# A two-layer hybrid backbone on one core: the first layer's modulation weights regrouped by feature, and its first four token tiles multiplied part by part

## The chip, the core and the metric

The kernel runs on one core of a Trainium2 chip. The metric is device microseconds (us) of one execution, and the number for a kernel is the median of its runs. All work is float32: each operand of a large matrix product is split into a rounded part `h` and the rest `l`, and a product is three matmuls (`h*h`, `h*l`, `l*h`).

## The reference

Two layers run over 1024 latent tokens and 256 context tokens of width 1024. What matters here is the start of the first layer: a modulation vector from the condition, a normalised and modulated input, and the projection that feeds three head groups.

```python
def hybrid_layer(x, xc, c, c_ctx, lp, lambda_init, rope_a, rope_b, ctx_out):
    mod = jax.nn.silu(c) @ lp['w_mod'] + lp['b_mod']            # 1024 -> 6 * 1024
    mod_c = jax.nn.silu(c_ctx) @ lp['w_mod'] + lp['b_mod']
    sh1, sc1, g1, sh2, sc2, g2 = [m[:, None] for m in jnp.split(mod, N_MOD, axis=-1)]
    h = modulate(rms_norm(x, lp['norm1_gain']), sh1, sc1)       # h * (1 + sc1) + sh1
    hc = modulate(rms_norm(xc, lp['norm1_gain']), sh1c, sc1c)
    aq, ak, av, bq, bk, bv, cx, cg = jnp.split(h @ lp['w_in'], split_pts, axis=-1)
    ...
```

`aq, ak, av` feed differential attention, `bq, bk, bv` windowed attention, `cx, cg` a gated linear recurrence (LRU). After them come an output projection, a second norm and a gated MLP. All of that is the same in both kernels.

## The kernel before, in words

Tokens lie along the free axis in three chunks `CH` (0 to 511, 512 to 1023, and the 256 context tokens); features lie in eight blocks of 128 partitions, `KC = 8`. `phase_a` (L432) does a layer's norm, projection and LRU. For the first layer it goes so:

- `load` (L442) brings x of chunk 1, eight transfers of 256 KB. `norm_scale` (L381) squares it on ACT (`nacc`, `nsq`, L364 and L367), adds the squares on DVE and POOL (L369, L390), sums over partitions with four small matmuls (`n_col`, L392), takes the power -1/2 on POOL (`nr`, L396) and spreads the result over partitions with four transposes into a PSUM bank (`n_bc`, L399).
- `mod_first` (L304) is called four times. A call loads four 512 KB tiles `wmod` (512 output columns for all 1024 inputs), multiplies them (L302), copies the result to SBUF (`m`, L313), transposes it (`mod_t`, L291), and writes four column blocks of the table `mods` with a reduction (L293) and an addition of the bias (L296). Columns 0 to 7 of `mods` are the shifts of the eight feature blocks, 8 to 15 their scales, so all four calls are needed before any block has both.
- `affine` (L345) makes `amul = (1 + scale) * gain` for all blocks with two DVE instructions (L353, L354).
- `norm_apply` (L402) makes, for each block of a chunk, `ntm` on DVE (L411: x times `amul` times `n_bc`), `hh` on ACT (L417, or L413 and L184), and the rest `hl` on DVE (L418) or, for blocks 1, 4 and 6, on POOL (L187).
- `weight` (L189) loads 512 KB into one of two buffers `raw`, rounds it on ACT (L184) and takes the rest on POOL (L187). The four weights `ws` of the group `wg2` and `wx` of the LRU go through it.
- `qkv` (L625) multiplies one tile of 128 tokens by `ws`: 24 matmuls of 512 columns into one of four PSUM banks `qkv_ps` (L636 to L638), then `qk_post` (L655) normalises and rotates the result on ACT, DVE and POOL (its first read of the bank on DVE is L670). `lru` (L543) makes `cx` with 72 matmuls in three pieces (L427 to L429), then convolves, gates and scans.

`lru_consts` (L515) computes, for both layers in `setup`, constants from the parameters: a chain of small DVE instructions in a buffer of the tag `raw`.

The order is not the written one: the whole of `phase_a` stands in a block that the framework schedules by its own timeline (L278), engine by engine. Every engine then takes its own list strictly in order.

Of the kernel before, what the change touches and what calls it, by code (L numbers as in the profile page):

```python
# [19 lines left out]
DEPTH = 2  # L20
# [45 lines left out]
def prep(i):  # L66
# [11 lines left out]
    out["wmod"] = i["w_mod"].reshape(L, 4, 2, P, 12, 512).transpose(0, 4, 1, 3, 2, 5).reshape(L, 12, 4, P, 1024)  # L78
# [92 lines left out]
class Build:  # L171
# [17 lines left out]
    def weight(self, src, n=1024):  # L189
        nc = self.nc  # L190
        raw = self.big.tile([P, 1024], F32, tag="raw", name="raw", bufs=2)
# [37 lines left out]
    def setup(self):  # L229
# [9 lines left out]
        mk = self.big.tile([P, 1024], F32, tag="raw", name="mask_f", bufs=2)  # L239
        nc.sync.dma_start(mk[:, 0:384], self.a["cst"][:, 132:516])  # L240
        self.hi(self.mask, mk[:, 0:384])
# [10 lines left out]
        for l in range(DEPTH):  # L252
            p = self.cst.tile([P, NPRM], F32, name=f"prm{l}")
            nc.sync.dma_start(p, self.a["prm"][l])
            self.prms.append(p)
            self.modl.append(self.cst.tile([P, 48, 2], F32, name=f"mods{l}"))
            self.lru_consts(l)
# [7 lines left out]
        self.ud = self.dr.tile([NF, P, T], F32, name="ud")  # L265

# [19 lines left out]
    def mod_out(self, l, nb, m4):  # L286

        nc = self.nc
        pt = self.ps_t("mod_t")
        for j in range(4):  # L290
            nc.tensor.transpose(pt[:, P * j:P * j + P], m4[:, P * j:P * j + P], self.ident)  # L291
        out = self.modl[l][:, 4 * nb:4 * nb + 4, :]
        nc.vector.tensor_reduce(out, pt.rearrange("p (j g r) -> p j r g", j=4, g=4)[:, :, 0:2, :], AX.X, ALU.add)  # L293
        o, n = PRM["bmod"]
        bm = self.prms[l][:, o + 4 * nb:o + 4 * nb + 4]
        nc.vector.tensor_tensor(out, out, bm.unsqueeze(2).to_broadcast([P, 4, 2]), ALU.add)  # L296
# [7 lines left out]
    def mod_first(self, l, nb):  # L304
        nc = self.nc
        ps = self.psp.tile([P, 512], F32, tag="p", name="mod_ps")
        for a in range(4):
            raw = self.big.tile([P, 1024], F32, tag="h", name="wmod", bufs=16)
            nc.sync.dma_start(raw, self.a["wmod"][l, nb, a])
            for s in range(2):  # L310
                self.mod_mm(ps, 2 * a + s, raw[:, 512 * s:512 * s + 512], a < 2, a >= 2)
        m4 = self.s5("m4")
        nc.scalar.activation(m4, ps, AF.Copy)  # L313
        self.mod_out(l, nb, m4)
# [30 lines left out]
    def affine(self, which, l=None):  # L345
        nc = self.nc
        l = self.l if l is None else l
        mods = self.modl[l]
# [1453 lines left out]
```

## Time and profile before

| | us |
|---|---|
| runs | 3084.51, 3085.17, 3091.09 |
| median | 3085.17 |
| the profiled execution | 3091.96 |
| its span, first to last instruction | 3089.4 |
| PE busy (share of the span) | 2840.6 (92%) |
| DVE busy | 2060.3 (67%) |
| ACT busy | 1450.4 (47%) |
| POOL busy | 1513.6 (49%) |

PE is the matrix engine, PEld its weight loads, DVE the vector engine, ACT the scalar engine, POOL the general engine, SP the one that issues nearly all transfers. The shares are means over the whole span; the change lies in its first 175 us, so the rows further down are of that stretch.

### The profile page before, as it was taken

The numbers are of one execution on the slowest core, as the hardware profiler recorded it, in microseconds if no ns is written. First come the engines' busy times: TensorE is split into PE (matmuls) and PEld (weight loads), VectorE is DVE, ScalarE is ACT, GpSimd is POOL, SyncE is SP. The second block draws the span as 40 slices with busy tenths as digits, with TensorE's granted clock in tenths as the row PEclk, the third lists the DMA queues.
The fourth block names the chain that finished last, engine by engine and source line by source line (L and its number), as shares of the span: only waits on it lengthen the run. The fifth ranks groups of instructions, "written<-read, shape, count | busy, mean of one in ns | idle before, by whom it ended". The sixth has DMA issues, their size and how long they took to land. (4 is left out here: it accounts for less than half of the span.)

```text
span 3089.4 us, 40964 instructions
## 1 busy us (share of the span) xinstructions
PE 2840.6 (92%) x15146; PEld 2307.3 (75%) x15146; DVE 2060.3 (67%) x2879; ACT 1450.4 (47%) x2410; POOL 1513.6 (49%) x1011
## 2 busy tenths in 40 slices
PE   6999798999899999998988989898999799999898
PEld 4798665768688888886777778666777678887776
DVE  6956556775855444457887884756885755555997
ACT  5444366785444344343332444466883444444331
POOL 4645412323555444439562664612323566665981
PEclk9999999999999999999999999899999999999999
DMA  7232636664121121143215341454534122224322
GB/s 252 81 85 79 167 67 219 196 212 158 51 81 67 68 74 67 67 169 125 82 49 200 103 113 52 118 135 148 138 118 146 55 82 82 84 85 159 122 83 82
DMA packets 208279, 349.25 MB, mean 113 GB/s; under 512 B 32720, under 2 KB 112336, under 8 KB 208080
## 3 DMA queue, kind: packets, MB, share of 16 engines
q1 hardware_dynamic: 203472, 331.69, 33.2%
q0 software_dynamic: 4608, 14.95, 2.2%
q8 instruction: 119, 1.95, 0.3%
q14 instruction: 80, 0.66, 0.1%
HBM read 257.19 MB, written 89.39 MB: 112 GB/s over the span
## 5 line engine op out<-in xcount | busy, mean ns | idle before, releaser
L184 ACT ACTIVATE w_r<-w_raw 128x512 fp32r<-128x512 f32 x338 | 213.0, 632 | 447.1 <-PE u_ps L1550 276.8
L1522 POOL TENSOR_TENSOR w_raw<-w_raw 128x512 f32<-128x512 f32 x176 | 250.9, 1430 | 226.8 <-DVE w_r L187 105.5
L187 DVE TENSOR_TENSOR w_r<-w_raw,w_r 128x512 fp32r<-128x512 f32 x206 | 149.4, 728 | 250.3 <-ACT w_r L184 250.2
L1549 PE MATMUL u_ps<-a,w_r 128*128 128x512 f32 x704 | 278.3, 396 | 5.2 <-DVE vb L1637 4.0
L1550 PE MATMUL u_ps<-a,w_r 128*128 128x512 f32 x704 | 277.5, 394 | 1.4 <-DVE a L187 1.2
L1551 PE MATMUL u_ps<-a,w_r 128*128 128x512 f32 x704 | 275.9, 392 | 0.0
L187 POOL TENSOR_TENSOR w_r<-w_raw,w_r 128x512 fp32r<-128x512 f32 x132 | 190.7, 1445 | 119.2 <-ACT w_r L184 114.0
L1401 PE MATMUL d_ps<-d_ah,d_b 128*128 128x512 f32 x560 | 224.7, 402 | 22.3 <-DVE xd L1378 10.9
L1402 PE MATMUL d_ps<-d_al,d_b 128*128 128x512 f32 x560 | 224.5, 401 | 6.2 <-DVE d_al L187 6.2
L1403 PE MATMUL d_ps<-d_ah,d_b 128*128 128x512 f32 x560 | 223.5, 399 | 0.7 <-DVE d_b L187 0.7
L944 DVE TENSOR_REDUCE da_sm<-da_s 128x1 f32<-128x1280 f32 (+1 forms) x144 | 194.9, 1368 | 42.8 <-PE da_s L934 42.0
L187 POOL TENSOR_TENSOR w<-raw,w 128x1024 fp32r<-128x1024 f32 (+2 forms) x62 | 140.7, 2276 | 145.1 <-ACT w L184 136.5
L951 ACT ACTIVATE da_e<-da_s,da_sm 128x1280 f32<-128x1280 f32 (+1 forms) x144 | 177.6, 1235 | 24.7 <-DVE da_sm L944 22.7
L1549 PEld LDWEIGHTS u_ps<-a,w_r 128*128 128x128 f32 x704 | 133.7, 190 | 34.8 <-DVE vb L1637 5.6
L1088 POOL TENSOR_TENSOR oy_x<-oy_x,oy_z 128x426 f32<-128x426 f32 (+3 forms) x48 | 52.1, 1085 | 217.6 <-ACT oy_z L1086 189.3
L1550 PEld LDWEIGHTS u_ps<-a,w_r 128*128 128x128 f32 x704 | 133.8, 190 | 29.7 <-DVE a L187 2.1
L1551 PEld LDWEIGHTS u_ps<-a,w_r 128*128 128x128 f32 x704 | 133.5, 190 | 28.6
L1378 DVE SCALAR_TENSOR_TENSOR xd<-d_ps,mods,xd 128x512 f32<-128x512 f32 x200 | 140.9, 741 | 18.9 <-PE d_ps L1403 18.8
L1401 PEld LDWEIGHTS d_ps<-d_ah,d_b 128*128 128x128 f32 x560 | 108.9, 195 | 47.7 <-issue 9.1
L934 PE MATMUL da_s<-dak,daq 96*128 96x512 f32 (+1 forms) x400 | 123.0, 395 | 14.9 <-ACT da_e L951 14.5
L1637 DVE TENSOR_TENSOR vb<-u_ps,vb 128x512 f32<-128x512 f32 x96 | 66.1, 688 | 99.4 <-PE u_ps L1551 90.5
L1402 PEld LDWEIGHTS d_ps<-d_al,d_b 128*128 128x128 f32 x560 | 108.9, 194 | 30.2 <-DVE d_al L187 8.0
(347 smaller groups left out, 8589.6 us busy)
## 6 DMA issues: line engine op xcount, KB each, us to landing
wmod<-in_wmod SPq DMA_DIRECT2D x96, 512.0 KB, 6.5
w_raw<-in_wu SPq DMA_DIRECT2D x44, 1024.0 KB, 5.4
d_w<-in_wd SPq DMA_DIRECT2D x40, 512.0 KB, 3.9
d_a<-ud SPq DMA_DIRECT2D x40, 512.0 KB, 4.7
ud<-conv SPq DMA_DIRECT2D x22, 640.0 KB, 2.9
ud<-conv SPq DMA_DIRECT2D x22, 512.0 KB, 2.6
raw<-in_wg SPq DMA_DIRECT2D x16, 512.0 KB, 4.4
dak<-qk_da POOLq DMA_DIRECT2D x48, 160.0 KB, 4.5
```

The costliest lines, as they stand in the source:

```text
L184: self.nc.scalar.activation(out, in_, AF.Copy)
L187: (eng or self.nc.vector).tensor_tensor(out, in_, hi.bitcast(F32), ALU.subtract)
L944: nc.vector.tensor_reduce(st["sm"][:, mi:mi + 1], st["s"][mi][:, :b["nkc"]], AX.X, ALU.max, negate=True)
L951: nc.scalar.activation(e[:, :nkc], st["s"][mi][:, :nkc], AF.Exp, bias=st["sm"][:, mi:mi + 1], accum_out=b["s0"][:, ti, u["hd"], mi:mi + 1])
L1378: nc.vector.scalar_tensor_tensor(x, ps, gate, x, ALU.mult, ALU.add)
L1401: nc.tensor.matmul(ps, bh[:, w], ah[:, m], start=on is None and k == 0, stop=False, **kw)
L1402: nc.tensor.matmul(ps, bh[:, w], al[:, m], start=False, stop=False, **kw)
L1403: nc.tensor.matmul(ps, bl[:, w], ah[:, m], start=False, stop=k == 1, **kw)
L1522: sub = lambda o, a, b, op=ALU.subtract: nc.gpsimd.tensor_tensor(o, a, b, op)
L1549: nc.tensor.matmul(ps, wh[:, s], h, start=new and kk == 0, stop=False, skip_group_check=not new)
L1550: nc.tensor.matmul(ps, wh[:, s], lo, start=False, stop=False, skip_group_check=not new)
L1551: nc.tensor.matmul(ps, wl[:, s], h, start=False, stop=kk == 3, skip_group_check=not new)
```

## The change

On the host the columns of the first eight groups of `w_mod` are put in another order, so that one `mod_first` call yields shift and scale of two feature blocks. Only a part (two blocks) is then finished at a time: `mod_first`, `affine_part`, `norm_apply` of those two blocks for chunk 1, and the 24 matmuls that these two blocks add to the four tiles of chunk 1, whose four PSUM banks stay open over the four parts. `mod_out` writes the first four groups in two pieces. The four `wg2` weights and `wx` are loaded between the `wmod` tiles (two through `raw`, two through a spare weight buffer `stage`), ahead of x of chunks 2 and 3. The norms of chunks 2 and 3 are written behind the four parts. The mask, the second layer's parameters and its `lru_consts` move from `setup` to behind the first group's tiles.

```diff
+    first = [8 * s + 2 * p + j for p in range(4) for s in range(2) for j in range(2)]
+    wm = i["w_mod"].reshape(L, D, 48, P)[:, :, first + list(range(16, 48))]
+    out["wmod"] = wm.reshape(L, 4, 2, P, 12, 512).transpose(0, 4, 1, 3, 2, 5).reshape(L, 12, 4, P, 1024)
...
+        for c0, i0, m in [(2 * nb, 0, 2), (8 + 2 * nb, 2, 2)] if nb < 4 else [(4 * nb, 0, 4)]:
+            out = self.modl[l][:, c0:c0 + m, :]
+            nc.vector.tensor_reduce(out, src[:, i0:i0 + m], AX.X, ALU.add)
+            bm = self.prms[l][:, o + c0:o + c0 + m]
+            nc.vector.tensor_tensor(out, out, bm.unsqueeze(2).to_broadcast([P, m, 2]), ALU.add)
...
-        for l in range(DEPTH):
...
+        self.setup_layer(0)
...
                 load(*CH[0])
+                ws = [self.qkv_weight("wg2", p) for p in range(2)]
+                stage = self.wt_tile("w_raw", F32)
                 pb = self.norm_scale(xt, *CH[0])
-                ws = []
-                weight = lambda: ws.append(self.qkv_weight("wg2", len(ws)))
-                for nb in range(4):
-                    self.mod_first(0, nb)
-                weight()
-                weight()
+                hh, hl, raws = [], [], []
+                am, bm = self.affine_out(1)
+                gbank = lambda name: psg.tile([P, 512], F32, tag="g", name=name)
+                first = [psp.tile([P, 512], F32, tag="p", name="qkv_ps") for _ in range(4)]
+                for p in range(4):
+                    raws.append([])
+                    for a in range(4):
+                        raws[p].append(self.big.tile([P, 1024], F32, tag="h", name="wmod", bufs=16))
+                        nc.sync.dma_start(raws[p][a], self.a["wmod"][0, p, a])
+                    if p < 2:
+                        ws.append(self.weight(self.a["wg2"][l, p + 2], raw=stage[:, 1024 * p:1024 * p + 1024]))
+                wx = self.weight(self.a["wc"][l, 0])
                 load(*CH[1])
                 load(*CH[2])
-                am, bm = self.affine(1)
-                hh = [self.h_tile(f"hh{j}") for j in range(KC)]
-                hl = [self.h_tile(f"hl{j}") for j in range(KC)]
-                self.norm_apply(xt, am, bm, hh, hl, *CH[0], pb, {3: weight, 6: weight})
+                for p in range(4):
+                    self.mod_first(0, p, raws[p], gbank)
+                    for j in range(2):
+                        hh.append(self.h_tile(f"hh{2 * p + j}"))
+                        hl.append(self.h_tile(f"hl{2 * p + j}"))
+                    self.affine_part(am, 1, 0, slice(2 * p, 2 * p + 2))
+                    self.norm_apply(xt, am, bm, hh, hl, *CH[0], pb, (2 * p, 2 * p + 1))
+                    for t in range(4):
+                        self.qkv_mm(first[t], t, 512, 0, ws, hh, hl, (2 * p, 2 * p + 1))
                 pbs = [self.norm_scale(xt, *c) for c in CH[1:]]
-                wx = self.weight(self.a["wc"][l, 0])
                 for c, pb in zip(CH[1:], pbs):
                     self.norm_apply(xt, am, bm, hh, hl, *c, pb)
...
-                pipe = self.qkv(grp, ws, n, range(4), hh, hl, psp) if j == 0 else []
+                pipe = self.qkv(grp, ws, n, range(4), hh, hl, psp, done=first) if j == 0 else []
+                if l == j == 0:
+                    self.setup_mask()
+                    self.setup_layer(1)
```

What the scheduler makes of it is not in the diff. Three places of the two programs' lists follow; a line number is that of the program it stands in, and numbers behind names tell tiles apart.

The start of SP's list after the first x transfers, before (`wmod` are the modulation weights, `raw<-in_wg` the weights of `wg2`):

```order
L444 DMA x_179<-in_xt 128x512
L309 DMA wmod<-in_wmod 128x1024 x16
L192 DMA raw<-in_wg 128x1024 x2
L444 DMA x_172<-in_xt 128x512
L444 DMA x_173<-in_xt 128x512
```

and now, with what each waits for beside other transfers (`DVE` and `Pool` are those engines):

```order
L458 DMA x_140<-in_xt 128x512 [waits DMAHW2_49]
L196 DMA raw<-in_wg 128x1024 [waits DMAHW3_49]
L196 DMA raw<-in_wg 128x1024 [waits DMAHW4_49,DVE_49]
L472 DMA wmod<-in_wmod 128x1024 [waits DMAHW5_49]
L472 DMA wmod<-in_wmod 128x1024 [waits DMAHW6_49]
```

Two `wg2` transfers now stand ahead of the 16 `wmod`, and the second of them waits for DVE. After eleven `wmod` come the other two `wg2` transfers, then the last five `wmod`, `wc`, and x of chunks 2 and 3.

PE from the end of part 0 (blocks `hh_283`, `hh_285`) to the start of part 1 (`hh_342`), now; before, all `mod_t` stand ahead of the first `qkv_ps`:

```order
L663 MATMUL qkv_ps<-w,hh_285 128x512
L664 MATMUL qkv_ps<-w,hh_285 128x512
L665 MATMUL qkv_ps<-w,hl_286 128x512 x4
L300 MATMUL mod_t<-cst_all,m_331 128x128 x4
L313 MATMUL mod_ps<-wmod,silu_c 32x512 x8
L663 MATMUL qkv_ps<-w,hh_342 128x512
```

The transposes of part 1 (`m_331`) stand behind the last matmul of part 0.

PE around the sums of chunk 2 (the second `n_col` of the list), before, where `hh_361` and `hh_362` are blocks 3 and 4 of chunk 1 and half of the first four tiles is still to do:

```order
L636 MATMUL qkv_ps<-w,hh_361 128x512
L637 MATMUL qkv_ps<-w,hh_361 128x512
L638 MATMUL qkv_ps<-w,hl_369 128x512
L392 MATMUL n_col<-one,nacc 128x1 x4
L636 MATMUL qkv_ps<-w,hh_362 128x512 x4
L399 MATMUL n_bc<-cst_all,nr 128x128 x4
```

and now, where `hh_461` is block 7:

```order
L665 MATMUL qkv_ps<-w,hl_462 128x512
L442 MATMUL cx_ps<-hl_460,w 128x428
L443 MATMUL cx_ps<-hh_459,w 128x428
L441 MATMUL cx_ps<-hh_461,w 128x428
L442 MATMUL cx_ps<-hl_462,w 128x428
L443 MATMUL cx_ps<-hh_461,w 128x428
L408 MATMUL n_col<-one,nacc 128x1 x4
L415 MATMUL n_bc<-cst_all,nr 128x128 x4
```

The sums of chunk 2 moved from the middle of the first four tiles to behind all of them and behind the first piece of `cx`. DVE's list fits this: the additions of chunk 2's squares (L385) follow `ntm` of block 7 of chunk 1, where before they stood between blocks.

## Rows read from the trace of the kernel before

**Rows 1.** Stretches: length, busy (instructions) by engine, PEclk, DMA share, GB/s

```profile
88.34:174.00 85.66, 78.07 (x354) 64.92 (x353) 70.22 (x97) 37.91 (x52) 61.14 (x40) 0.96 0.36 99
174.00:311.00 137.00, 136.93 (x658) 118.50 (x656) 84.47 (x94) 62.81 (x79) 63.17 (x30) 1.00 0.27 77
```

**Rows 2.** Timeline of PE: start, us, engine, line, operation, count [idle before <- its end]

```profile
88.34 0.39 PE L636 MATMUL qkv_ps<-w,hh 128*128 128x512 f32 x1
...
174.00 0.33 PE L636 MATMUL qkv_ps<-w,hh 128*128 128x384 f32 x1
```

**Rows 3.** Timeline of PE, the first 60 us

```profile
19.94 1.93 PE L302 MATMUL mod_ps<-wmod,silu_c 128*32 128x512 f32 x8
21.80 1.11 PE L399 MATMUL n_bc<-cst_all,nr 128*128 128x128 f32 x4
...
28.80 1.93 PE L302 MATMUL mod_ps<-wmod,silu_c 128*32 128x512 f32 x16
...
34.73 0.66 PE L291 MATMUL mod_t<-cst_all,m 128*128 128x128 f32 x4 [0.72 <-ACT m L313]
41.96 2.08 PE L636 MATMUL qkv_ps<-w,hh 128*128 128x512 f32 x4 [6.58 <-ACT hh L417]
...
57.18 1.02 PE L392 MATMUL n_col<-one,nacc 128*128 128x1 f32 x8 [2.27 <-DVE nacc L390]
```

**Rows 4.** Timeline of DVE

```profile
11.85 1.34 DVE L535 TENSOR_TENSOR spw<-spw 128x6 f32<-128x6 f32 x2
...
35.42 0.19 DVE L293 TENSOR_REDUCE mods<-mod_t 128x8 f32<-128x32 f32 x1 [2.83 <-PE mod_t L291]
...
35.85 2.22 DVE L353 TENSOR_SCALAR amul<-mods 128x16 f32<-128x16 f32 x1
...
61.30 3.38 DVE L411 SCALAR_TENSOR_TENSOR ntm<-x,amul,n_bc 128x512 f32<-128x512 f32 x5 [1.62 <-PE n_bc L399]
...
82.62 0.48 DVE L418 SCALAR_TENSOR_TENSOR hl<-ntm,mods,hh 128x256 fp32r<-128x256 f32 x1
...
85.98 0.69 DVE L670 TENSOR_TENSOR qa<-qkv_ps,qr 128x512 f32<-128x512 f32 x1 [0.40 <-POOL qr L668]
```

**Rows 5.** Timeline of ACT

```profile
3.78 0.52 ACT L184 ACTIVATE mask_r<-mask_f 128x384 fp32r<-128x384 f32 x1 [0.80 <-DMA mask_f<-in_cst]
...
34.08 0.60 ACT L313 ACTIVATE m<-mod_ps 128x512 f32<-128x512 f32 x1 [2.63 <-PE mod_ps L302]
...
41.19 0.72 ACT L417 ACTIVATE hh<-ntm,mods 128x512 fp32r<-128x512 f32 x1 [4.62 <-DVE ntm L411]
```

**Rows 6.** Transfers by line, 69 to 75 us: count, KB each, us to landing

```profile
raw<-in_wg SPq DMA_DIRECT2D x2, 384.0 KB, 3.0
```

**Rows 7.** Stretches, columns as in group 1: `wmod` loads; after PE's idle time at 55

```profile
20.00:30.00 10.00, 9.24 (x49) 2.95 (x52) 0.88 (x5) 1.20 (x2) 1.03 (x1) 1.00 1.03 410
62.00:64.00 2.00, 1.87 (x4) 1.49 (x5) 2.00 (x5) 1.44 (x2) 2.00 (x2) 0.50 0.44 98
```

**Rows 8.** Timeline of POOL

```profile
35.70 4.64 POOL L187 TENSOR_TENSOR w<-raw,w 128x1024 fp32r<-128x1024 f32 x2 [14.38 <-ACT w L184]
...
58.72 1.02 POOL L396 TENSOR_TENSOR nr<-nv,mhalf 128x4 f32<-128x4 f32 x1
...
66.84 2.41 POOL L187 TENSOR_TENSOR w<-raw,w 128x1024 fp32r<-128x1024 f32 x1 [2.41 <-ACT w L184]
```

**Rows 9.** DVE by line and shape, 61.3 to 83.1 us: count, busy us, mean ns, idle before

```profile
L418 DVE SCALAR_TENSOR_TENSOR hl<-ntm,mods,hh 128x512 fp32r<-128x512 f32 x5 | 8.9, 1790 | 1.3 <-ACT hh L417 1.3
L411 DVE SCALAR_TENSOR_TENSOR ntm<-x,amul,n_bc 128x512 f32<-128x512 f32 x8 | 5.6, 740 | 1.6 <-PE n_bc L399 1.6
```

**Rows 10.** Stretches of `qkv_ps`, then of `cx_ps` alone: length, busy (count) of PE first

```profile
46.40:54.90 8.50, 8.50 (x38) 6.70 (x36) 0.00 (x0) 0.00 (x0) 1.00 0.69 194
...
74.14:88.50 14.36, 14.35 (x72) 13.30 (x71) 1.05 (x2) 1.00 0.14 42
156.50:163.30 6.80, 6.78 (x22) 6.21 (x22) 0.53 (x1) 0.61 0.28 77
```

More of the change, by code (lines that the diff above doesn't have):

```diff
@@ L302, in mod_mm, with mod_first @@
         self.nc.tensor.matmul(ps[r:r + 32, :], self.sl[:, 2 * k:2 * k + 32], w, start=start, stop=stop, tile_position=(0, r))
-    def mod_first(self, l, nb):
+    def mod_first(self, l, nb, raws, bank):
         nc = self.nc
[L306 to L311, printed above, removed]
+        ps = bank("mod_ps")
+        for k in range(KC):
+            self.mod_mm(ps, k, raws[k // 2][:, 512 * (k % 2):512 * (k % 2) + 512], k < 4, k >= 4)
         m4 = self.s5("m4")
         nc.scalar.activation(m4, ps, AF.Copy)
-        self.mod_out(l, nb, m4)
+        self.mod_out(l, nb, m4, bank)
     def mod_units(self, todo):
@@ L400, in norm_scale, with norm_apply @@
         return pb
-    def norm_apply(self, xt, am, bm, hh, hl, o, n, pb, between={}):
+    def norm_apply(self, xt, am, bm, hh, hl, o, n, pb, js=range(KC)):
         nc = self.nc
         s = 0 if o < NLAT else 1
-        for j in range(KC):
-            if j in between:
-                between[j]()
+        for j in js:
             tm = self.s5("ntm")[:, :n]
@@ L623, in qkv_weight, with qkv_mm, qkv @@
         return self.weight(self.a[grp][self.l, kk], 768 if grp == "wg3" else 1024)
-    def qkv(self, grp, ws, n, tiles, hh, hl, psp, pipe=()):
+    def qkv_mm(self, ps, t, n, c0, ws, hh, hl, ks=range(KC)):
+        nc = self.nc
+        tok = slice(P * t, P * t + P)
+        for k in ks:
+            wh, wl = ws[k // 2]
+            cs = slice(n * (k % 2) + c0, n * (k % 2) + n)
+            nc.tensor.matmul(ps[:, c0:n], hh[k][:, tok], wh[:, cs], start=(k == 0), stop=False)
+            nc.tensor.matmul(ps[:, c0:n], hh[k][:, tok], wl[:, cs], start=False, stop=False)
+            nc.tensor.matmul(ps[:, c0:n], hl[k][:, tok], wh[:, cs], start=False, stop=(k == KC - 1))
+    def qkv(self, grp, ws, n, tiles, hh, hl, psp, pipe=(), done=None):
         nc = self.nc
@@ L628, in qkv @@
         for t in tiles:
-            ps = psp.tile([P, 512], F32, tag="p", name="qkv_ps")
-            tok = slice(P * t, P * t + P)
             c0 = 256 if self.last and t >= 8 and grp != "wg3" else 0
-            for k in range(KC):
-                wh, wl = ws[k // 2]
-                cs = slice(n * (k % 2) + c0, n * (k % 2) + n)
-                nc.tensor.matmul(ps[:, c0:n], hh[k][:, tok], wh[:, cs], start=(k == 0), stop=False)
-                nc.tensor.matmul(ps[:, c0:n], hh[k][:, tok], wl[:, cs], start=False, stop=False)
-                nc.tensor.matmul(ps[:, c0:n], hl[k][:, tok], wh[:, cs], start=False, stop=(k == KC - 1))
+            if done:
+                ps = done[t]
+            else:
+                ps = psp.tile([P, 512], F32, tag="p", name="qkv_ps")
+                self.qkv_mm(ps, t, n, c0, ws, hh, hl)
             if grp == "wg3":
```

57 lines of the change are left out of this document (32 added, 25 removed).

## The prediction

> **What bounds the kernel now.** I read the stretches of the page's first 311 us, then the timelines of PE and DVE there, then single lines. After 174 us PE is busy 136.93 of 137 us [rows 1]: whatever the start saves or loses by then, PE passes on. So the question is only when PE reaches the first matmul of the next group, at 174.00 [rows 2]. Between 88.34 us, where PE takes up the fifth token tile [rows 2], and 174 us PE is busy 78.07 of 85.66 us and DVE 70.22 [rows 1]: two engines near their limit, each feeding the other. Before that come three marks. PE's first product of the projection starts at 41.96 us, after 6.58 us without work [rows 3]. DVE's norms of chunks 2 and 3 run from 61.30 us (it waited for `n_bc`) to 83.10 us (82.62 + 0.48) [rows 4]. And DVE's first read of a finished tile is at 85.98 us [rows 4]. The reader is to see two clocks here: PE's, which the change puts forward, and DVE's, which must reach the norms of chunks 2 and 3 for PE to have anything more to do.
>
> **The change, step by step.** All times are on the profiled execution (3091.96 us, span 3089.4); it lies 6.8 us over the median 3085.17, and I put the difference onto the median.
>
> *Transfers.* Two `wg2` weights (512 KB each) now stand ahead of the 16 `wmod`. The second waits for DVE, because its `raw` buffer first holds the first layer's LRU constants. That chain now ends 13.2 us into the span (11.85 + 1.34) for two interleaved layers [rows 4]; for one layer each instruction still needs the one before, so it is no shorter, but it starts about 1 us earlier, the 0.80 us wait and 0.52 us copy of `mask_r` being gone from ACT [rows 5]. I take 12.3 us for its end, and 3.0 us to the landing with an idle queue [rows 6]: 15.3 us. From there a 512 KB load takes 1.28 us (524 KB at 410 GB/s [rows 7]): part 0's four `wmod` are in at 20.4 us, the last of them, with the other two `wg2` among them, at 38.4 us. x of chunk 2 follows until about 46 us. Bounds: 1 us either way for the wait.
>
> *Part 0.* Its `n_col` come first on PE and end about 20.5 us, as now (POOL's two weight rests of 2.3 us [rows 8] sit beside DVE's last addition). Then eight modulation matmuls, four of which took 1.93 us there (two records each), and `n_bc`, 1.11 us [rows 3], end at 25.4; `m` takes 0.60 [rows 5], `mod_t` 0.7 [rows 3], six tiny DVE instructions 1.1 (an estimate from 0.19 for one [rows 4]), `ntm` 0.74 [rows 9], `hh` 0.72 [rows 5]. First product: about 29.4 us, 12.5 us earlier than now.
>
> *PE through the four parts.* 96 matmuls at 0.224 us (38 in 8.50 [rows 10]) are 21.5 us; 24 of `cx` at 0.2 (72 in 14.36 [rows 10]) 4.8; 18 modulation matmuls left, eight in 1.93 us by then [rows 3], 4.3; three `mod_t` of 0.66 2.0. Together 32.6. The gaps: `mod_t` of part 1 stands behind all of part 0, so the tiny instructions, `ntm` and `hh` of part 1 (1.1 + 0.74 + 0.72) lie bare but for eight modulation matmuls: 0.7 us of gap. To it comes POOL. Two weight rests meet the tiny DVE instructions of part 1 just then; a tiny `amul` beside such a rest took 2.22 us [rows 4] where POOL's pair ran 35.70 to 40.34 [rows 8], so I add 2.0 us (bounds 0 and 2.3). Part 2's chain is covered, part 3's by 18 matmuls of `cx` but for 0.7, since its block 6 passes ACT twice. PE is through with the first four tiles and the first piece of `cx` at 29.4 + 32.6 + 3.4 = 65.4 us. Today that point is 74.14 + 4.8 = 78.9 us: PE is 13.5 us ahead.
>
> The Trainium skill, "SBUF — State Buffer", section "Who interferes with whom", speaks against the change here: the vector engine's instructions with two SBUF inputs, and `tensor_scalar`, share a port pair with GpSimd and block fully, while a reduction never does. The rows agree (2.22 us for 16 columns); without the rule the sum would be 2.0 us less, and the wait is more often met, since the four tiny instructions now run four times.
>
> *DVE to the norms of chunk 2.* The `n_col` of chunk 2 stand behind all this on PE, where they were in the middle of the first four tiles. Behind 65.4 us come 1.02 for `n_col` [rows 3], 0.2 for `nv`, 1.02 for `nr` [rows 8] and, half of the 1.11 at the higher clock, 0.5 for `n_bc`: the norms start at 68.1 us, 6.8 us later than now. DVE could not be much sooner: `ntm` of the last two blocks waits for part 3's `mod_t`, and the additions for chunk 2's squares stand behind it. The second layer's parameters, read by DVE ahead of the last addition, land near 54 us and hold nothing.
>
> *The norms.* Now they take 21.8 us. Five `hl` of 512 columns took 1.79 us each where `ntm` took 0.74 [rows 9]: 5.2 us beyond, beside 1.3 us of waiting for ACT; POOL had four weight rests there (one is 66.84 for 2.41 [rows 8]) and three `hl` of its own. Three of the rests are gone, the `hl` remain, so I take half of the 6.5 us off: 18.5 us, bounds 15.3 and 21.8. They end at 86.6, 3.5 us later than now. The second layer's constants, hidden in DVE's idle first 13 us until now, add 31 tiny instructions after 60 us; most fall into waits, I count 0.6 us, at most 5.
>
> *The first tiles out.* DVE's first read comes at 85.98 + 3.5 + 0.6 = 90.1 us. PE can then start the fifth tile 0.7 us behind it, at 90.8 instead of 88.34: 2.5 us later. PE's lead is gone, spent waiting for norms.
>
> *88 to 174 us.* The same instructions in another order: the scheduler now puts the LRU's convolutions and scans ahead of tiles. PE loses 7.6 us there now by waits [rows 1] and about 2.4 us by the clock (22 `cx` in 6.80 us instead of 4.4 [rows 10]). I cannot price the new order row by row; between losing nothing (-10) and losing twice (+10) I take +1, since the fifth tile is alone before the first gates. Sum: 2.5 + 1 = **3.5 us later** at 174 us, and so at the end.
>
> *The rest.* The regrouped weights have the same loads. The first four groups of the second layer's modulation get two more tiny DVE instructions each beside attention: eight at 0.2, so 1.6 us if PE's work there did not cover DVE; 0 taken. The mask's load and copy only move: its 0.52 us on ACT falls beside squares that DVE is behind with; 0 taken, 0.5 if not.
>
> **The rivals.**
>
> *PE's lead survives (faster).* If PE set the pace up to 88 us as it nearly does behind it (7.6 us of waits in 85.66 [rows 1]), 13.5 us of lead would count. It needs the norms of chunk 2 to end by about 78 us, so to start near 60: no bare gaps in the parts, no POOL wait. For it: DVE waits 1.62 us for `n_bc` at 61.30 [rows 4], so today it could start sooner. Against: PE's own list holds `n_col` behind 32.6 us of work. A lead of 5 us at the norms and half of the 10 us lost later saved give 3085 - 10 = 3075 us. A half of it is the low end.
>
> *The clock (slower).* After 2.27 us without work [rows 3] and some thin work PE ran at a granted 0.50, its 1.2 GHz level [rows 7], and at a mean of 0.61 the 22 `cx` took 6.80 us [rows 10]. The new order has one such gap at part 1, thin work from 66 to 88 us, and a wait at the fifth and sixth tiles; if each brings the lower level and 2.4 us, the sum is 3.5 + 7.2 = 10.7 us: 3096 us. It decides where the gaps come up to that 2.27 us; mine at part 1 is 2.7. The Trainium skill, "TensorE: Matmul & The Clock Gate", Part 1, has it that the lower level is the default and activity lifts it, which fits these rows.
>
> *Nothing is put forward (no change).* Transfers could hold PE until 38 us as they hold it now; then DVE's clock stays and the time with it. It gives the same number as the forecast within its range and counts there.
>
> **How the numbers follow.** No change to be told, 3.5 us later or near it, has 0.50: PE's lead is certain, its use is not. The faster rival has 0.17, the clock and what else delays the norms 0.33. A measurement of this kernel tells 0.2% (6.2 us) from nothing. Predicted: 3085.2 + 3.5 = 3088.7 us. The bounds of the steps (1 for the transfer, 2 for POOL, 3.2 for the norms, some 5 for the later order) lie within 7 us either way; with half of the faster rival and all of the slower one the range is 3079 to 3099; the forecast's own is 3083 to 3095.
>
> **What would show it.** Right: the first `qkv_ps` near 29 us; a gap near 2.7 us before part 1; the first four tiles done near 62 us; `n_bc` of chunk 2 at 68 and the norms over at 86 or 87; the fifth tile near 91; first matmul of 384 columns at 175 to 180; no idle PE from there. Wrong: norms of chunk 2 from 60 us, or the fifth tile before 86, and the first matmul of 384 columns before 170; or PE at 0.50 through most of the parts.

## The result: 0.9% slower, and the time is lost in two places

| | before | changed |
|---|---|---|
| median, us | 3086.68 (4 runs, 3084.51 to 3091.09) | 3114.67 (4 runs, 3108.34 to 3116.76) |
| ratio, 95% interval | | 1.0090 [1.0078, 1.0102] |
| the profiled execution, its span | 3091.96, 3089.4 | 3116.76, 3115.0 |

The change costs 28.0 us; the forecast was 3.5 us later, range 3079 to 3099. The traces show nearly all of it in the first 200 us. The stretches of the changed kernel, from its fifth tile on (columns as in [rows 1]):

```profile
101.17:197.89 96.72, 81.18 (x359) 65.74 (x358) 73.67 (x102) 38.74 (x53) 62.98 (x40) 0.95 0.36 101
197.89:335.00 137.11, 136.12 (x653) 117.64 (x651) 87.56 (x94) 62.65 (x79) 63.97 (x30) 1.00 0.24 71
```

Against [rows 1], the fifth tile starts 12.8 us later (101.17 for 88.34), and the stretch from there to the unbroken products of 384 columns is 11.1 us longer (96.72 for 85.66), with PE idle for 15.5 us instead of 7.6. Behind that PE is busy for 136.12 of 137.11 us, so nothing is won back. Two losses, then: one ahead of the fifth tile and one behind it. PE's timeline for the first:

```profile
31.76 0.50 PE L663 MATMUL qkv_ps<-w,hh 128*128 128x512 f32 x1 [0.64 <-ACT hh L431]
...
43.35 0.63 PE L663 MATMUL qkv_ps<-w,hh 128*128 128x512 f32 x1 [2.34 <-ACT hh L431]
...
59.75 0.60 PE L300 MATMUL mod_t<-cst_all,m 128*128 128x128 f32 x4
...
65.31 0.50 PE L663 MATMUL qkv_ps<-w,hh 128*128 128x512 f32 x1 [1.44 <-ACT hh L187]
...
72.21 0.95 PE L408 MATMUL n_col<-one,nacc 128*128 128x1 f32 x8
75.48 0.65 PE L415 MATMUL n_bc<-cst_all,nr 128*128 128x128 f32 x4 [2.31 <-POOL nr L412]
...
79.43 0.72 PE L441 MATMUL cx_ps<-hh,w 128*128 128x426 f32 x1 [2.96 <-ACT hh L431]
...
101.17 0.46 PE L663 MATMUL qkv_ps<-w,hh 128*128 128x512 f32 x1
...
110.72 0.66 PE L736 MATMUL qk_t<-cst_all,qa 128*128 128x128 f32 x4 [3.83 <-DVE qa L731]
...
197.89 0.34 PE L665 MATMUL qkv_ps<-w,hl 128*128 128x384 f32 x1
```

PE's lead is real: the first product comes at 31.76 us instead of 41.96 [rows 3]. But `n_bc` of chunk 2 comes at 75.48; in the kernel before it came at 60.21:

```profile
60.21 1.05 PE L399 MATMUL n_bc<-cst_all,nr 128*128 128x128 f32 x4
```

From 72.40 to 101.17 us PE is busy for only 16.1 of 28.8 us. DVE shows why:

```profile
51.22 1.27 DVE L432 SCALAR_TENSOR_TENSOR hl<-ntm,mods,hh 128x512 fp32r<-128x512 f32 x1 [1.41 <-ACT hh L431]
60.38 0.26 DVE L305 TENSOR_REDUCE mods<-mod_t 128x4 f32<-128x16 f32 x2 [7.89 <-PE mod_t L300]
...
62.60 2.28 DVE L385 TENSOR_TENSOR nacc<-nacc,nsq 128x512 f32<-128x512 f32 x3
...
74.17 0.15 DVE L410 TENSOR_SCALAR nv<-n_col 128x4 f32<-128x4 f32 x1
...
75.50 2.25 DVE L563 TENSOR_TENSOR spw<-spw 128x6 f32<-128x6 f32 x1
77.79 0.17 DVE L564 TENSOR_SCALAR spw<-spw 128x6 f32<-128x6 f32 x1
77.87 1.41 DVE L425 SCALAR_TENSOR_TENSOR ntm<-x,amul,n_bc 128x512 f32<-128x512 f32 x2
...
98.07 0.47 DVE L432 SCALAR_TENSOR_TENSOR hl<-ntm,mods,hh 128x256 fp32r<-128x256 f32 x1
...
100.38 0.69 DVE L709 TENSOR_TENSOR qa<-qkv_ps,qr 128x512 f32<-128x512 f32 x1 [1.17 <-POOL qr L707]
101.93 0.94 DVE L594 TENSOR_SCALAR xc<-cx,prm 128x1280 f32<-128x1280 f32 x1 [0.86 <-ACT cx L586]
...
113.46 0.69 DVE L709 TENSOR_TENSOR qa<-qkv_ps,qr 128x512 f32<-128x512 f32 x1 [0.54 <-POOL qr L707]
...
184.61 0.68 DVE L709 TENSOR_TENSOR qa<-qkv_ps,qr 128x512 f32<-128x512 f32 x1
```

DVE stands for 7.89 us before 60.38, waiting for part 3's `mod_t`, which PE does only behind part 2's products (59.75). The additions of chunk 2's squares (62.60) stand behind that wait, although x of chunk 2 was in at 46.4 us. So the norms of chunk 2 begin at 77.87 instead of 61.30 [rows 4], 16.6 us later, and DVE's first read of a tile at 100.38 instead of 85.98, 14.4 us later. Between 30 and 60 us DVE is busy for 11.20 us; before it was 21.34 (first the changed kernel's stretch, then that of the kernel before):

```profile
30.00:60.00 30.00, 27.02 (x127) 16.69 (x122) 11.20 (x23) 11.47 (x17) 9.81 (x5) 0.94 0.88 286
30.00:60.00 30.00, 19.04 (x92) 13.42 (x85) 21.34 (x30) 19.19 (x33) 14.64 (x11) 0.88 0.77 244
```

The second loss: DVE's ten reads of the first group's tiles span 84.2 us (100.38 to 184.61), where before they spanned 74.1. What DVE waited for between first and last read, the three largest of 13.4 us in the changed kernel (us in total, times, longest):

```profile
DVE qa L709 <- POOL qr L707: 6.9, 7, 1.5
DVE qv L704 <- ACT qa L702: 2.6, 2, 1.4
DVE qa L190 <- ACT qb L187: 1.4, 1, 1.4
```

and in the kernel before all of its waits there, 5.0 us:

```profile
DVE qa L670 <- POOL qr L668: 4.2, 6, 0.9
DVE qa L692 <- POOL qa L688: 0.8, 2, 0.4
```

One read of the order stands out: the second tile is read 13.1 us behind the first (113.46), and the first convolution of the LRU (`xc`, from 101.93) has been put between them. Before, the second read came 4.6 us behind the first, and the convolution after it:

```profile
90.55 0.69 DVE L670 TENSOR_TENSOR qa<-qkv_ps,qr 128x512 f32<-128x512 f32 x1 [0.90 <-POOL qr L668]
91.16 1.84 DVE L562 TENSOR_SCALAR xc<-cx,prm 128x1280 f32<-128x1280 f32 x1
```

The 3.83 us that PE waits at 110.72 are for the first tile's rotated result (`qa`, L731), which stands behind parts of the convolution in DVE's list. With four banks, PE's sixth tile also needs the second read, and it starts right behind that read, at 114.35.

Three theories. **A**: the scale of chunk 2 (squares, additions, `n_col`, `n_bc`) stands behind the four parts in every list, so DVE starts its 20 us of norms late, and PE's early products are worth nothing. **B**: the second layer's LRU constants, now in DVE's list between 70 and 99 us, are the main loss. **C**: the place of the convolution costs some 10 us by itself.

### The profile page after: what moved, and what is told of

The parts are those of the page before. It is cut to its first block, busy times and chain, and to the rows that moved or that the text cites. A ratio compares the mean times of both kernels' runs of the same rounds, so it can differ in the third digit from the quotient of the medians.

```text
span 3115.0 us, 40974 instructions
## 1 busy us (share of the span) xinstructions
PE 2847.6 (91%) x15146; PEld 2312.7 (74%) x15146; DVE 2068.0 (66%) x2901; ACT 1449.5 (47%) x2410; POOL 1513.2 (49%) x1011
## 4 chain that ended last, share of the span: by engine, by line
PE 50%; DVE 13%; POOL 5%; issue 5%; ACT 3%; DMA 2%; SPq 0%; POOLq 0%; DVEq 0%; ACTq 0%
PE u_ps L1588 8%; PE u_ps L1589 8%; PE u_ps L1590 8%; DVE xd L1417 2%; DVE d_al L190 2%; PE c_ps L1601 1%; PE c_ps L1600 1%; PE c_ps L1599 1%; PE d_ps L1440 1%; PE d_ps L1442 1%; PE d_ps L1441 1%; PE da_pv L789 1%; PE sw_t L883 1%; ACT da_e L990 1%; PE o_ps L442 1%
## 5 line engine op out<-in xcount | busy, mean ns | idle before, releaser
L1440 PE MATMUL d_ps<-d_ah,d_b 128*128 128x512 f32 x560 | 222.9, 399 | 24.9 <-DVE a L1449 12.9
L1440 PEld LDWEIGHTS d_ps<-d_ah,d_b 128*128 128x128 f32 x560 | 107.8, 193 | 50.2 <-issue 11.8
L1676 DVE TENSOR_TENSOR vb<-u_ps,vb 128x512 f32<-128x512 f32 x96 | 66.1, 688 | 99.4 <-PE u_ps L1590 89.8
```

What stands on the lines that cost most here:

```text
L1440: nc.tensor.matmul(ps, bh[:, w], ah[:, m], start=on is None and k == 0, stop=False, **kw)
```

## The experiments

Times are compared with runs of the kernel before on the same chip. "First 384" is the start of the unbroken products of 384 columns. For its differences the second trace of the kernel before is taken (170.52; see e9). The columns of places come from one profiled execution of each run, the medians from 4 to 12 executions, so they need not agree to the microsecond.

| run | norms of chunk 2 start | first read | ten reads span | first 384, later by | median, later by | ratio, 95% interval |
|---|---|---|---|---|---|---|
| before | 61.30 | 85.98 | 74.1 | 3.5 | | |
| changed | 77.87 | 100.38 | 84.2 | 27.4 | 28.0 | 1.0090 [1.0078, 1.0102] |
| e1 | 76.05 | 98.07 | 80.2 | 23.3 | 26.4 | 1.0086 [1.0072, 1.0099] |
| e2 | 68.73 | 94.39 | 74.1 | 10.5 | 9.2 | 1.0029 [1.0020, 1.0038] |
| e3 | 75.34 | 97.90 | 85.1 | 25.8 | 30.6 | 1.0103 [1.0089, 1.0117] |
| e4 | 59.09 | 87.26 | 74.8 | 2.8 | 6.0 | 1.0019 [1.0010, 1.0028] |
| e5 | 75.81 | 98.32 | 75.7 | 14.5 | 15.8 | 1.0050 [1.0037, 1.0063] |
| e6 | 71.53 | 94.27 | 76.9 | 11.8 | 7.1 | 1.0022 [1.0013, 1.0031] |
| e7 | 65.02 | 87.56 | 75.1 | 3.5 | 4.8 | 1.0013 [1.0004, 1.0021] |
| e8 | 65.51 | 86.11 | 74.3 | 1.0 | 4.2 | 1.0014 [1.0006, 1.0023] |
| e9 | 61.32 | 85.26 | 74.1 | 0 | 0.5 | 1.0003 [0.9995, 1.0012] |
| e10 | 61.96 | 86.12 | 76.4 | 0.5 | 2.9 | 1.0008 [0.9999, 1.0016] |
| e11 | 66.00 | 90.46 | 66.1 | 9.6 | 4.4 | 1.0020 [1.0010, 1.0030] |
| e12 | 59.45 | 83.67 | 75.4 | 1.3 | -0.7 | 1.0000 [0.9989, 1.0011] |

**e1, the constants back in the set-up.**

```diff
-        self.setup_layer(0)
+        self.setup_mask()
+        self.setup_layer(0)
+        self.setup_layer(1)
...
-                if l == j == 0:
-                    self.setup_mask()
-                    self.setup_layer(1)
```

> The changed kernel (3114.7 us) with the second layer's parameters and LRU constants and the mask back in the set-up, as before the change; all else is the change's. Theory A (the scale of chunk 2 stands behind the four parts in every list, so the norms of chunks 2 and 3 and DVE's first read of a tile come 14 to 16 us late): only the tiny instructions between the last addition and the norms go, about 0.9 us before nv and 2.0 us before the first ntm, and the wait of part 0 gets about 1 us longer; 2 to 4 us faster than the change, near 3112. Theory B (the tiny instructions of the constants in DVE's list from 70 to 99 us are the main loss): 10 us or more faster, at or below 3104. Theory C (the order of the tiles and the LRU behind 101 us costs 10 us of its own): the stage from the fifth tile to the last product of 384 columns stays near 95 us.

1.6 us better than the change by the differences to the kernel before (26.4 for 28.0), which is within the noise, and 2.3 us at the first read. Theory B falls; A's price for the constants, 2 to 4 us, is near. The stretch to the first 384 columns stays at 94.7 us (99.09 to 193.78), as C said. But here the second read comes 7.3 us behind the first (105.38), not 13.1, and the stretch is hardly shorter: the second read alone does not make its length.

**e2, the scale of chunks 2 and 3 written ahead of part 3.**

```diff
                 for p in range(4):
+                    if p == 3:
+                        pbs = [self.norm_scale(xt, *c) for c in CH[1:]]
                     self.mod_first(0, p, raws[p], gbank)
...
-                pbs = [self.norm_scale(xt, *c) for c in CH[1:]]
```

> The changed kernel with one piece of code moved: the squares, additions and column sums of chunks 2 and 3 are written ahead of part 3 instead of behind it, so that DVE does them in its idle time between 44 and 60 us. Theory A: n_bc of chunk 2 comes right behind part 2 or within part 3, norms from about 66 us instead of 77.9, DVE's first read of a tile near 90 us instead of 100.4: 8 to 12 us faster than the change if the later stage keeps its length (3103 to 3107), and about 20 us faster (3094) if the later stage also goes back to 86 us. Theory B: no more than 2 us faster. Theory C: the first 10 us come, the other 10 do not.

18.8 us better than the change by the differences (9.2 for 28.0). DVE's timeline:

```profile
53.47 4.58 DVE L385 TENSOR_TENSOR nacc<-nacc,nsq 128x512 f32<-128x512 f32 x3 [0.71 <-ACT nsq L383]
...
68.73 1.39 DVE L425 SCALAR_TENSOR_TENSOR ntm<-x,amul,n_bc 128x512 f32<-128x512 f32 x2
...
94.39 0.69 DVE L710 TENSOR_TENSOR qa<-qkv_ps,qr 128x512 f32<-128x512 f32 x1 [0.23 <-POOL qr L708]
...
99.90 0.69 DVE L710 TENSOR_TENSOR qa<-qkv_ps,qr 128x512 f32<-128x512 f32 x1
```

The additions have moved into the idle time (53.47 instead of 62.60), the norms start 9.1 us earlier, and the first read comes 6.0 us earlier. The scheduler, working from this other start, also puts the second read back close behind the first (99.90), and the ten reads span 74.1 us again, 10.1 less: one edit, but both losses in it. Theory A's larger number held, though the norms came 2.7 us and the first read 4.4 us later than it had them, so part of that agreement is luck. What is left of the loss, 9.2 us, is near the lateness of the first read (8.4).

**e3, the products written behind all parts.**

```diff
                     self.norm_apply(xt, am, bm, hh, hl, *CH[0], pb, (2 * p, 2 * p + 1))
-                    for t in range(4):
-                        self.qkv_mm(first[t], t, 512, 0, ws, hh, hl, (2 * p, 2 * p + 1))
                 pbs = [self.norm_scale(xt, *c) for c in CH[1:]]
+                for t in range(4):
+                    self.qkv_mm(first[t], t, 512, 0, ws, hh, hl)
```

> The changed kernel without the contraction by parts: loads, regrouped modulation weights and norms by parts as in the change, but the 96 products of the first four tiles are written behind all parts and behind the scales of chunks 2 and 3, as before the change. Theory A: n_bc of chunk 2 comes near 62 us, the norms and DVE's first read of a tile are within 4 us of the kernel before (61.3 and 86.0), and the time is 3087 to 3097. If instead PE's early products were worth something to the change, this kernel is slower than the change, 3118 or more. Theory B: still at 3104 or above, since the constants stay where they are.

The edit did not do what it says. The scheduler put the products back between the parts (first product at 31.26 us, part 3's `mod_t` at 57.21), so this is the change once more, with the same loss. By the number alone (3115.6 us) it would have spoken against theory A; the order on PE says that it tests nothing. e6 does it over with a bond.

**e4, the kernel before with the constants and the mask late**, the reverse of e1's edit, applied to the kernel before.

> The kernel before (3086.7 us) with one part of the change alone: the mask and the second layer's parameters and LRU constants are written behind the first four tiles. Theory A: the 31 tiny instructions cost at most 3 us, 3085 to 3090. Theory B: 10 us or more slower than before, 3097 or above. Nothing of theory C is in it unless the scheduler's order changes by so little.

6.0 us slower [3.1, 8.6], 1 us above theory A's range and 6 us under theory B's. The first read is 1.3 to 2.0 us later than in the two traces of the kernel before. With e1 the constants cost some 2 to 6 us: more than the forecast's 0.6, far from the whole. (Both edits move the mask with them.)

**e5, the convolution held behind the second read.**

```diff
+            with ExitStack() as hold:
+                if l == j == d == 0:
+                    hold.enter_context(self.tc.issue_after(self.rd[1].ins))
-            nc.vector.tensor_scalar(xc, cx, wk(3), col(cb), ALU.mult, ALU.add)
+                nc.vector.tensor_scalar(xc, cx, wk(3), col(cb), ALU.mult, ALU.add)
```

`issue_after` adds an order between instructions of one engine and no wait; `self.rd` lists the first reads of the tiles.

> The changed kernel (3114.7 us) with one bond added to the order: the first convolution of the LRU stands behind the second tile's read in DVE's list, as in the kernel before, where the change has it right behind the first. Nothing ahead of 100 us differs. Theory C (this order makes the stage 10 us longer: PE has no free bank for the sixth tile until the second tile is read at 113.5): second read near 106 instead of 113.5, ten reads in 75 to 79 us instead of 84, 6 to 10 us faster than the change, 3105 to 3109. Rival (the stage is long because of waits on POOL and ACT that any order has): within 2 us of the change.

12.2 us better than the change (15.8 for 28.0), somewhat more than the 6 to 10 expected. DVE's timeline:

```profile
98.32 0.69 DVE L713 TENSOR_TENSOR qa<-qkv_ps,qr 128x512 f32<-128x512 f32 x1 [1.17 <-POOL qr L710]
...
105.63 0.69 DVE L713 TENSOR_TENSOR qa<-qkv_ps,qr 128x512 f32<-128x512 f32 x1 [0.90 <-POOL qr L710]
106.24 0.94 DVE L597 TENSOR_SCALAR xc<-cx,prm 128x1280 f32<-128x1280 f32 x1
```

The ten reads span 75.7 us instead of 84.2: theory C holds for 8.5 us, with one reserve. Up to the first read all four engines have the changed kernel's lists; behind the second read the scheduler put many other instructions elsewhere too, so the 8.5 us are the price of the order that the bond leads to, not of one place alone. The first read is 2 us earlier too, which the bond can't do; 1.6 of that is the clock in part 1 (last section). Together 10.6, near the 12.2. The stretch from the fifth tile to the first 384 columns shows what went:

```profile
99.22:185.04 85.82, 77.23 (x353) 63.37 (x353) 68.98 (x102) 37.76 (x53) 63.05 (x40) 0.98 0.34 89
```

Against 96.72 us in the changed kernel, PE's idle time fell by 7.0 us (15.5 to 8.6) and its own work by 3.9 (81.18 to 77.23). Of the 3.9, 0.9 are five products that the changed kernel does ahead of the mark; the granted clock rose from 0.95 to 0.98. So a part of what the bond won back, some 3 us (an estimate from these two rows), was the lower clock.

**e6, the early products taken away, the scale put forward.**

```diff
                 for p in range(4):
                     self.mod_first(0, p, raws[p], gbank)
+                    if p == 3:
+                        pbs = [self.norm_scale(xt, *c) for c in CH[1:]]
...
-                    for t in range(4):
-                        self.qkv_mm(first[t], t, 512, 0, ws, hh, hl, (2 * p, 2 * p + 1))
-                pbs = [self.norm_scale(xt, *c) for c in CH[1:]]
+                with tc.issue_after(self.last_t.ins):
+                    for p in range(4):
+                        for t in range(4):
+                            self.qkv_mm(first[t], t, 512, 0, ws, hh, hl, (2 * p, 2 * p + 1))
```

`self.last_t` is the last `mod_t` transpose written so far, part 3's here.

> The change with its early products taken away and the scale put forward: all 96 products of the first four tiles stand behind part 3's modulation on PE, and the squares, additions and column sums of chunks 2 and 3 are written between part 3's modulation and its norms. First product near 41 us instead of 31.8, part 3's mod_t near 41 instead of 59.8. Theory A (DVE's way to the norms of chunk 2 decides, PE's early products are worth nothing): norms of chunk 2 from 62 to 65 us, first read 86 to 90 us, and the time 3085 to 3094, no slower than the run with the scale alone put forward (3094.3). Rival (the early products save PE time that counts): slower than that run, 3100 or more, although the norms come earlier.

PE's timeline shows the bond at work, later than expected, since part 3's `mod_t` itself came only at 48.10:

```profile
48.10 0.66 PE L300 MATMUL mod_t<-cst_all,m 128*128 128x128 f32 x4 [2.41 <-ACT m L321]
48.51 0.48 PE L666 MATMUL qkv_ps<-w,hh 128*128 128x512 f32 x1
```

The first product is 16.5 us later than in e2 (48.51 for 32.02), and the time is not worse: 7.1 us over the kernel before, e2 9.2, the intervals overlapping. So the early products are worth nothing that can be measured, which was the point. The norms came later than expected (71.53): the column sums waited behind products on PE, `nv` came at 65.26, and `n_bc` stood behind more products, until 70.89. The time lies in the expected range although the norms were over 6 us later than expected.

**e7 and e8, three edits at once, and one more.** e7 is e1, e2 and e5 together. e8 is e7 with the products of part p behind the modulation of part p + 1:

```diff
+                def products(p):
+                    with tc.issue_after(self.last_t.ins):
+                        for t in range(4):
+                            self.qkv_mm(first[t], t, 512, 0, ws, hh, hl, (2 * p, 2 * p + 1))
...
                     self.mod_first(0, p, raws[p], gbank)
+                    if p:
+                        products(p - 1)
```

> The change with three edits at once: scale of chunks 2 and 3 written ahead of part 3 (worth 20 us by itself), second layer's constants and mask back in the set-up (worth 3 us by itself), and the first convolution behind the second tile's read. If they add: 3114.7 - 20 - 3 = 3091, and the convolution adds nothing since that order was there already when the scale alone was put forward. Theory A with the constants out of the norms of chunks 2 and 3: norms from 67 us, over 20 us later, first read near 90 us, 3 to 5 us later than before: 3088 to 3092. If it comes out at 3084 or less, the early products do have a use once the norms are not held up.

> The edits of the run before (scale ahead of part 3, constants in the set-up, convolution behind the second read) and one more: the products of each part stand behind the modulation of the next part on PE, so that DVE's norms of a part run beside PE's products of the part before. mod_t of part 1 near 32 us instead of 38.6, of part 2 near 41 instead of 46.8, part 3's waits for the column sums of chunk 2, which wait for chunk 2's squares. Theory A: what counts is when the norms of chunk 2 start. If its x (landed at 46.4) and the squares on ACT set that, the norms start near 62 and the time is 3084 to 3089; if nothing comes earlier than in the run before, the same time as there.

e7: 4.8 us over the kernel before, inside its range; 23.2 of the 28.0 us are gone with the contraction by parts still in place. So most of the loss lay in the order. e8: 4.2 us, no different from e7. Its first read is level with the kernel before (86.11) and its first 384 columns come 1.0 us later; where the rest of the 4.2 us lies is not shown.

**e9, the kernel before again.**

> The kernel before once more, unchanged, for a second trace of it. All comparisons by stage rest on one trace of the kernel before, whose execution took 3091.96 us where the median is 3085 to 3087. In every run so far the median stood 2 to 8 us further from the kernel before than the start of the products of 384 columns (174.00 us in that trace) does, by 5 us on average, in the run with the constants alone 6.7. If that trace was late by chance in its first 174 us, this one shows the first product of 384 columns near 169 us; if it is near 174 again, something behind it is slower in all variants. Time: no difference from the kernel before, 3085.

Level, as it must be. Its products of 384 columns start at 170.52 us, 3.5 us ahead of the first trace, so the first trace was late by chance, for 2.3 us of it by the clock in one place (last section):

```profile
170.52 0.33 PE L636 MATMUL qkv_ps<-w,hh 128*128 128x384 f32 x1
```

Against this trace the changed kernel's fifth tile is 14.5 us later (86.70 here) and the stretch from there 12.9 us longer (83.82 here); PE has 7.3 us more idle time in it and 5.6 more of its own work, 0.9 of it the five products. Against this trace also, the column "first 384" agrees with the column of medians within 5 us in every run (in e11, where 24 of these products were done ahead, with 4 us taken off for them).

**e10, e11, e12, attempts to be faster than both.** All three keep e8's edits and load x of chunk 2 ahead of the weights of parts 2 and 3. The scale of chunk 2 is written behind part 2's modulation in e10 and e12, ahead of it in e11.

```diff
                 for p in range(4):
+                    if p == 2:
+                        load(*CH[1])
...
                     self.mod_first(0, p, raws[p], gbank)
+                    if p == 2:
+                        pbs.append(self.norm_scale(xt, *CH[1]))
...
+                products(3, n_bc2)
```

> What the runs so far suggest, put together: as in the last run (constants in the set-up, products of a part behind the modulation of the next, convolution behind the second read), and x of chunk 2 is loaded ahead of the weights of parts 2 and 3 (2 MB, 5.1 us, so the last of those weights land near 44 us instead of 38.7), its scale is written ahead of part 2, the products of part 3 stand behind its n_bc, and the weight of cx and x of chunk 3 are loaded last. Theory A: x of chunk 2 lands near 34 us, its scale is ready when part 3's modulation is, near 50 us, and the norms of chunk 2 start at 50 to 55 us instead of 61.3 in the kernel before; first read 76 to 80 us instead of 86.0, and the time 6 to 10 us under the kernel before, 3075 to 3079. Rival: ACT and the six shared small buffers hold the squares and norms of both chunks up, and the norms still start at 60 us or later: 3085 or above.

> The run before (x of chunk 2 ahead of the weights of parts 2 and 3) had the scale of chunk 2 on hand too late again: its x was in at 35.0 us, but its squares stood behind part 2's modulation in ACT's list (41.8), and its n_bc behind part 2's products in PE's (61.3, though the column sums were done at 50.9). Here the scale of chunk 2 is written ahead of part 2's modulation, part 2's products stand behind n_bc, the weight of cx is loaded ahead of x of chunk 3, and the third piece of cx has a bank that does not wait for ACT. Theory A: n_bc of chunk 2 near 46 us; part 3's modulation then ends last, near 52, and the norms of chunk 2 start at 54 to 56 us, 6 us earlier than in the kernel before (61.3); first read 78 to 81 instead of 85.3 to 86.0; first product of 384 columns 164 to 168 instead of 170.5; 3079 to 3083, 2 to 6 us under the kernel before. Rival (PE, which must still do the products of 96 and 72 matmuls, or the weights of part 3, hold the norms of the last two blocks to 60 us): no difference from before.

> The order of the run e10 (scale of chunk 2 written behind part 2's modulation, x of chunk 2 loaded ahead of the weights of parts 2 and 3, x's squares from 41.8 us, column sums done at 50.9), with two edits: the products of parts 2 and 3 stand behind n_bc of chunk 2 on PE (in e10, n_bc came at 61.3 because part 2's products stood ahead of it), and the weight of cx is loaded ahead of x of chunk 3. The third piece of cx keeps its bank. Theory A: n_bc of chunk 2 near 56 us behind 18 matmuls of cx, norms of chunk 2 from about 57 instead of 61.3 to 62.0, first read 81 to 82 us, first product of 384 columns 166 to 168 instead of 170.5 to 171.0: 3080 to 3084, 2 to 4 us under the kernel before. If it is no faster than the kernel before although the norms start near 57, DVE's way to the norms is no longer what decides, and the limit lies in the norms and the tiles themselves.

None beats the kernel before. In e10 PE had the column sums done at 50.91 us, but `n_bc` stood behind part 2's products in its list and came at 61.27. In e11 PE waited 3.60 us for the additions with part 2's `mod_t` queued behind them, so everything of parts 2 and 3 moved back (part 3's `mod_t` at 59.05). e12 got the norms to 59.45 and the first read to 83.67, 1.6 to 2.3 us ahead of the kernel before, where 81 to 82 was expected. But its third read is at 100.23, where the kernel before has it at 100.41 and 101.13, so the lead is gone two tiles later, and the time is level, 1.0000 [0.9989, 1.0011]:

```profile
56.82 0.60 PE L417 MATMUL n_bc<-cst_all,nr 128*128 128x128 f32 x4
```

Here `n_bc` no longer held the norms; DVE's list did, with the rest of part 3, the additions of chunk 3 and two short waits in it. What sets the pace behind the second read these runs do not show.

## Why the prediction was wrong, step by step

- **Transfers: right.** The last `wmod` landed at 38.7 us (38.4 expected), x of chunk 2 at 46.4 (about 46 expected).
- **Part 0: 2.4 us late.** First product 29.4 expected, 31.76 measured. The forecast had POOL's two weight rests beside DVE's last addition and put nothing for it. The addition took 2.71 us, where before it took 0.69 without them, so `n_col` ended about 2 us late:

```profile
17.95 2.71 DVE L406 TENSOR_TENSOR nacc<-nacc 128x512 f32<-128x512 f32 x1
15.02 5.09 POOL L190 TENSOR_TENSOR w<-raw,w 128x1024 fp32r<-128x1024 f32 x2 [0.41 <-ACT w L187]
```

- **PE through the four parts: mis-sized by 7.0.** 65.4 us expected, 72.4 measured. 2.4 us are the late start. The gaps were near: 3.4 us expected, 3.8 measured. The 2.34 us ahead of part 1 came as forecast, with two additions of four columns that took 1.95 us instead of 0.24 beside POOL's rests; the 1.44 us ahead of part 3 came because its `hh` stood behind the squares on ACT. PE's own work took 36.9 us instead of 32.6. The first eight matmuls of part 1 ran at a granted 0.54 and took 0.43 us each instead of 0.224, which is 1.6 us; the other 2.7 are spread over many small steps (two modulation matmuls between products took 1.0 us, not 0.5).
- **DVE to the norms of chunk 2: the step that failed.** It put the norms at 68.1 us; they began at 77.87. Of these 9.8 us, 7.0 are PE's later end, since the forecast let `n_col` wait for all parts. The other 2.8 lie between: from the end of the parts to the norms it took 5.5 us, not 2.7, because constants and additions of chunk 3 stood ahead of `nv`, and one 6-column instruction of the constants took 2.25 us (75.50). The forecast also said that "DVE could not be much sooner", from the list alone. That was wrong: DVE stood idle for 7.89 us with the additions behind the wait, and e2, which moved that code, had the norms 9.1 us and the first read 6.0 us earlier.
- **The norms: in bounds.** 18.5 expected, bounds 15.3 to 21.8; 20.7 measured (77.87 to 98.54). The 20.7 hold 3.02 us of a table (`tab`, 95.13) that before stood behind the norms; without it they are 17.7, in bounds too.
- **The first tiles out:** 90.1 and 90.8 expected, 100.38 and 101.17 measured; the difference is the later start of the norms.
- **88 to 174 us: the second step that failed, mis-sized by 10.** +1 taken, between -10 and +10; the stretch took 11.1 us more than in [rows 1]. I wrote that the scheduler now put convolutions ahead of tiles and did not price it. e5 did, with the order that its bond leads to: 10.9 us off the stretch, 8.5 off the ten reads. The rows to read were in the trace of the kernel before: two tiles read 4.6 us apart ahead of the convolution, and four banks.
- **The rest: right.** Nothing clear of the scatter shows behind 198 us. The constants (0.6 counted, at most 5) cost 2 to 6 us.

Together: the fifth tile 10.4 us later than forecast, the stretch behind it 10.1 longer, and 3.5 us by which the trace that both are counted from was late itself. That is 24.0 of the 24.5 us that the forecast missed.

The rivals: PE's lead did not survive. The clock rival's number (3096) came nearest. Its lower level did come: 0.54 at part 1, 0.50 from 83.18 to 87.68 us, 0.63 from 110.70 to 115.00. But it is a small part of the loss: about 2 us at the first read, nothing at 83 us, since PE waited again behind it (4.03 us at 94.99, for ACT), and 3 to 5 us in the stretch behind the fifth tile. Its condition, gaps that come up to 2.27 us, did not decide: e5 had a gap of 2.32 us ahead of part 1 and kept 1.00. Nothing of the third rival is true; work was put forward by 10 us. No case had two order effects of over 8 us adding up, so the range ended 16 us short.

## What to carry to other kernels

When work is put forward on an engine, look in the other engines' lists at what now stands behind the waits that this makes: an engine that waits is no free time if the work that could fill it is queued behind the wait. A scheduler that orders by its own timeline can move an operation far downstream when the start moves, so compare the order of the scarce engine (here DVE, with four banks behind it) all the way to where both orders meet, and price each swap. A bond that moves one instruction lets such a scheduler move others behind it, so what it gains is the price of the whole new order. Before an edit to written order is taken as an experiment, see on the engine that the order moved.

## What was unexpected of the hardware

- **The same work at two clocks.** Part 1 of the changed kernel and of e5 has the same 2.3 us gap ahead of it and the same matmuls behind. In the changed kernel the granted clock over its first eight was 0.54, near the level of 1.2 GHz; in e5 it was 1.00, and the part took 7.4 us instead of 8.9. First the changed kernel's eight matmuls, then the whole part in e5:

```profile
43.30:46.80 3.50, 3.45 (x9) 2.56 (x10) 1.50 (x2) 1.09 (x2) 0.00 (x0) 0.54 1.03 357
```

```profile
43.00:50.30 7.30, 7.30 (x36) 4.82 (x40) 4.67 (x11) 3.82 (x6) 1.44 (x2) 1.00 0.99 302
```

  So it was with the kernel before: the 22 `cx` that took 6.80 us at 0.61 [rows 10] took 4.5 us in e9 at a granted 1.00, in this stretch:

```profile
155.40:160.00 4.60, 4.60 (x27) 4.44 (x26) 4.28 (x5) 2.40 (x3) 4.60 (x3) 1.00 0.20 57
```

  I had taken that slow stretch as a property of the order. It was one execution's, worth 2.3 us, and one trace can't tell the two apart. The Trainium skill, "TensorE: Matmul & The Clock Gate", Part 1, has it for the start of a kernel that the count of matmuls at the lower level varies between runs of one kernel. The two traces of the kernel before show the same in its middle: 22 of them in this stretch, and none. What decided it each time no run here shows.

- **A 6-column instruction of 2.25 us.** The `spw` product at 75.50 normally takes 0.17 us, as the product at 75.10 did. POOL's rest of a weight runs from 75.39 to 77.73:

```profile
75.39 2.34 POOL L190 TENSOR_TENSOR w<-raw,w 128x1024 fp32r<-128x1024 f32 x1
```

  The Trainium skill, "SBUF — State Buffer", section "Who interferes with whom", has it that a vector instruction with two SBUF inputs contends with a GpSimd instruction that reads SBUF, and that the lock is exclusive. The trace agrees: 2.25 us beside 2.34. The forecast used the rule for `amul` at part 1 and not for the constants, which put many such instructions next to the norms.
